# A running log-sum-exp over 4096 rows: Exp taken three chunks ahead of Ln, the last totals and the last store moved, small DMAs issued by GpSimd

## The chip, the core and the metric

The kernel runs on one core of one Trainium2 chip. The metric is device time in microseconds (us), the median of several runs. TensorE is called PE, VectorE DVE, ScalarE ACT, GpSimd POOL and SyncE SP, as in the profile.

## What is computed

The input x is 4 batches of 4096 rows of 4128 numbers (float32). Row t of the output is the log-sum-exp of rows 0 to t of the same batch, element by element:

```python
out[:, 0, :] = x[:, 0, :]
for t in range(1, S):
    mx = np.maximum(out[:, t - 1, :], x[:, t, :])
    out[:, t, :] = mx + np.log(np.exp(out[:, t - 1, :] - mx) + np.exp(x[:, t, :] - mx))
```

The kernel computes it as Ln of the running sum of Exp(x). That is good only as long as the sums stay in range, so it also works out a flag from the totals of all columns; only if the flag is 0 is everything done again by a slow general path. With these inputs the general path is not run.

## The kernel before

**Steps.** A batch's 4096 rows are cut into steps of 384 rows (3 rows for each of 128 partitions) and one of 256 rows (2 for each partition): ten of the one and one of the other, the short one first in batch 0 and last in the others. There are 44 steps, 0 to 43; the last one is short. A step is loaded into a buffer `xt` of 128 x 3 x 4128 by one DMA, worked on in place, and stored by one DMA. There are four buffers (`BUFS`). All loads (L87) and stores (L90) are issued by SyncE, in this order: loads 0 to 3, store 0, store 1, load 4, store 2, load 5 and so on, and at the end stores 41, 42 and 43. A load waits until the store of the step that had its buffer has landed.

**Chunks.** The columns of a step are worked on in four chunks, three of 1024 and one of 1056. The 176 chunks are numbered through. Each passes these operations:

- `exp` (L108, ACT): Exp of all its rows, in place.
- `sums` (L112, DVE): adds each partition's first row to its second and the second to the third.
- `head` (L119, PE): a matrix product with a triangle of ones (`excl`) gives each partition the sum of the partitions before it, added in PSUM (`base`) to what earlier steps left there. For the fourth chunk `head_rest` (L127, L129) does so in three pieces, with the earlier steps' sum from `carry`.
- `add` (L143) or `add_rest` (L136), DVE: adds that base to all rows.
- `pass_on` (L152, PE): puts the last partition's last row, the running total, into `base` for the next step; for the fourth chunk `keep` (L148, DVE) copies it to `carry`.
- `ln` (L164, ACT): Ln in place. It has to wait for `pass_on` or `keep`, which still read the sums.
- `total` (L159, DVE): after the last step of a batch, a chunk's totals are summed into a column of `part`.

**Order.** The order on every engine is written out by hand (`manual_schedule`), in one loop over the chunks. Round g does `sums` and `head` of chunk g + 1, `add` and `pass_on` of chunk g, `exp` of chunk g + 2, and `ln` of chunk g; behind the fourth chunk of a step stand its store and a later load. The rounds after the last step of a batch also hold the totals of the chunk before. So ScalarE alternates Exp of a chunk with Ln of the second chunk before it, and every engine takes its instructions strictly in order.

**The small loads.** Four DMAs, issued by ScalarE (L183), bring row 0 of each batch into a tile `first`, 32 partitions for each batch; at half of the loop its Exp(-x) is summed into the last column of `part` (L217).

**The end.** `part` is summed (L226), the partitions by a matrix product (L228), and compared with a limit (L229). All engines read the flag (L284) and branch (L285). The general path (L250 to L268) has its loads and stores on SyncE.

Of the kernel before, what the change touches and what calls it, by code (L numbers as in the profile page):

```python
# [7 lines left out]
FP32 = mybir.dt.float32  # L8
INT32 = mybir.dt.int32
ACT = mybir.ActivationFunctionType  # L10
AX = mybir.AxisListType
ALU = mybir.AluOpType
P = 128
R = 3
CH = 1024
MM = 512
BUFS = 4
HI = 96
LIMIT = float(2 ** 40)
STEPS = 15  # L20


def _constants(nc, pool):

    def triangle(base, name):
        t = pool.tile([P, P], FP32, name=name)
        nc.gpsimd.memset(t, 1.0)
        nc.gpsimd.affine_select(
            out=t, in_=t, pattern=[[1, P]], compare_op=ALU.is_ge,
            fill=0.0, base=base, channel_multiplier=-1,  # L30
        )
        return t

    excl = triangle(-1, "excl")
    pick = pool.tile([P, P], FP32, name="pick")
    nc.gpsimd.memset(pick, 0.0)
    nc.gpsimd.affine_select(  # L37
        out=pick, in_=pick, pattern=[[0, P]], compare_op=ALU.not_equal,
        fill=1.0, base=-(P - 1), channel_multiplier=1,
    )  # L40
    ones = pool.tile([P, 1], FP32, name="ones")
    nc.gpsimd.memset(ones, 1.0)
    return excl, pick, ones


def _fast(ctx, tc, x, out, flag):


    nc = tc.nc
    B, S, D = x.shape  # L50
# [6 lines left out]
    excl, pick, ones = _constants(nc, consts)  # L57
    xpool = ctx.enter_context(tc.tile_pool(name="xpool", bufs=BUFS))
    cpool = ctx.enter_context(tc.tile_pool(name="cpool", bufs=1))
# [1 line left out]
    prest = ctx.enter_context(tc.tile_pool(name="prest", bufs=2, space=bass.MemoryType.PSUM))  # L61

    carry = cpool.tile([P, rest], FP32, name="carry")
    q = P // B
    first = cpool.tile([P, D // q], FP32, name="first")
    part = cpool.tile([P, 4 * B + 1], FP32, name="part")
    every = cpool.tile([P, 1], FP32, name="every")
    nc.vector.memset(carry, 0.0)  # L68
# [5 lines left out]
    class Step:  # L74
        def __init__(self, b, row, r):
            self.b, self.row, self.r = b, row, r
            self.first = row == 0
            self.last = row + P * r == S
# [7 lines left out]
            self.xt = full[:, :self.r, :]  # L86
            nc.sync.dma_start(out=self.xt, in_=self.dram(x))  # L87

        def store(self):
            nc.sync.dma_start(out=self.dram(out), in_=self.xt)  # L90

    class Chunk:
        def __init__(self, step, c):
            self.t, self.c = step, c
            self.a = c * CH
            self.w = CH if c < 3 else rest
            self.end = c == 3
            self.q = {}

        def rows(self, lo, hi):  # L100
            return self.t.xt[:, lo:hi, self.a:self.a + self.w]
# [2 lines left out]
            return self.t.xt[:, j, self.a:self.a + self.w]  # L104

        def exp(self):
            rows = self.rows(0, self.t.r)
            nc.scalar.activation(rows, rows, ACT.Exp)  # L108

# [37 lines left out]
        def keep(self):  # L147
            nc.vector.tensor_copy(carry[HI:P, :], self.row(self.t.r - 1)[HI:P])  # L148

# [6 lines left out]
        def total(self):  # L156
            own = carry if self.end else base[self.c]
            i = 4 * self.t.b + self.c
            nc.vector.tensor_reduce(  # L159
                out=part[HI:P, i:i + 1], in_=own[HI:P, :self.w], axis=AX.X, op=ALU.add)  # L160

# [5 lines left out]
    for b in range(B):  # L167
        n = S // P
# [9 lines left out]
    chunks = [Chunk(s, c) for s in steps for c in range(4)]  # L178
    n = len(chunks)
    for s in steps[:BUFS]:  # L180
        s.load()
    for b in range(B):
        nc.scalar.dma_start(  # L183
            out=first[b * q:(b + 1) * q, :], in_=x[b, 0, :].rearrange("(q f) -> q f", q=q))
    stored = 0
    chunks[0].exp()
    chunks[1].exp()
    chunks[0].sums()
    chunks[0].head()
    for g, k in enumerate(chunks):  # L190
        after = chunks[g + 1] if g + 1 < n else None
        if k.end:
            k.add_rest(0)
            for i in range(2, len(subs)):
                k.head_rest(i)
            for i in range(1, len(subs)):
                k.add_rest(i)
            k.keep()
            if after:
                after.sums()  # L200
                after.head()
        else:
            after.sums()
            if after.end:
                after.head_rest(0)
                after.head_rest(1)
            else:
                after.head()
            k.add()
            k.pass_on()  # L210
        if g + 2 < n:
            chunks[g + 2].exp()
        k.ln()
        if g and chunks[g - 1].t.last:
            chunks[g - 1].total()
        if g == n // 2:
            nc.scalar.activation(  # L217
                first, first, ACT.Exp, scale=-1.0, accum_out=part[:, 4 * B:4 * B + 1])
        if k.end:
            k.t.store()  # L220
            if BUFS <= stored + BUFS - 1 < len(steps):
                steps[stored + BUFS - 1].load()
            stored += 1

    chunks[-1].total()
    nc.vector.tensor_reduce(out=every, in_=part, axis=AX.X, op=ALU.add)  # L226
    q = prest.tile([P, MM], FP32, name="q")
    nc.tensor.matmul(q[:1, :1], lhsT=every, rhs=ones, start=True, stop=True)  # L228
# [3 lines left out]
def _general(ctx, tc, x, out):  # L232

    nc = tc.nc
    B, S, D = x.shape
    q = P // B
    f = D // q
    assert P == B * q and D == q * f and (S - 1) % STEPS == 0
    one = ctx.enter_context(tc.tile_pool(name="one", bufs=1))
    state = one.tile([P, f], FP32, name="state")  # L240
    xs = one.tile([P, STEPS, f], FP32, name="xs")
    os = one.tile([P, STEPS, f], FP32, name="os")
    mx = one.tile([P, f], FP32, name="mx")
    two = one.tile([P, 2, f], FP32, name="two")

    def flat(t, b, first, n):
        return t[b, bass.ds(first, n), :].rearrange("t (q f) -> q t f", q=q)

    for b in range(B):
        nc.sync.dma_start(out=state[b * q:(b + 1) * q, :].unsqueeze(1), in_=flat(x, b, 0, 1))  # L250
    for b in range(B):
        nc.sync.dma_start(out=flat(out, b, 0, 1), in_=state[b * q:(b + 1) * q, :].unsqueeze(1))
    with tc.For_i(1, S, STEPS) as i:
        for b in range(B):
            nc.sync.dma_start(out=xs[b * q:(b + 1) * q], in_=flat(x, b, i, STEPS))
        for j in range(STEPS):
            own = state if j == 0 else os[:, j - 1, :]
            nc.vector.tensor_tensor(out=mx, in0=own, in1=xs[:, j, :], op=ALU.max)
            nc.vector.tensor_tensor(out=two[:, 0, :], in0=own, in1=mx, op=ALU.subtract)
            nc.vector.tensor_tensor(out=two[:, 1, :], in0=xs[:, j, :], in1=mx, op=ALU.subtract)  # L260
            nc.scalar.activation(two, two, ACT.Exp)
            nc.vector.tensor_tensor(
                out=two[:, 0, :], in0=two[:, 0, :], in1=two[:, 1, :], op=ALU.add)
            nc.scalar.activation(two[:, 0, :], two[:, 0, :], ACT.Ln)
            nc.vector.tensor_tensor(out=os[:, j, :], in0=mx, in1=two[:, 0, :], op=ALU.add)
        nc.vector.tensor_copy(state, os[:, STEPS - 1, :])
        for b in range(B):
            nc.sync.dma_start(out=flat(out, b, i, STEPS), in_=os[b * q:(b + 1) * q])  # L268


@with_exitstack
def kernel(
    ctx: ExitStack,
    tc: tile.TileContext,
    x: bass.AP,
    out: bass.AP,
):
    nc = tc.nc
    nc.scalar.preload_act_table_set("natural_log_exp_and_others")  # L279
    flags = ctx.enter_context(tc.tile_pool(name="flags", bufs=1))  # L280
    flag = flags.tile([1, 1], INT32, name="flag")
    with ExitStack() as inner:
        _fast(inner, tc, x, out, flag)
    good = nc.values_load(flag, min_val=0, max_val=1, skip_runtime_bounds_check_because="a comparison gives 0 or 1")  # L284
    with tc.If(good == 0, preferred_fallthrough_block=False):  # L285
        with ExitStack() as inner:
            _general(inner, tc, x, out)
# [30 lines left out]
```

## Time and profile before

| | us |
|---|---|
| median of 3 runs | 1272.1 (1271.65 to 1272.37) |
| profiled execution, device time | 1271.84 |
| its span, first to last instruction | 1270.1 |
| busy: DVE, ACT, PE | 1033.2, 929.3, 799.2 |
| load or store of a 3-row step | 6192 KB |
| load or store of a 2-row step | 4128 KB |

| work of a 3-row step | row | instructions x mean us |
|---|---|---|
| Exp | L108 | 3 x 2.75 and 1 x 2.83 |
| Ln | L164 | 3 x 2.76 and 1 x 2.83 |
| sums | L112 | 6 x 1.22 and 2 x 1.26 |
| add | L143 | 3 x 3.35 |
| add_rest | L136 | 2 x 1.75 and 1 x 0.25 |
| carry copy | L148 | 1 x 0.71 |

How to read the views: busy time is what an engine spent in instructions; the share of an engine says nothing of what sets the end. The DMA share is that of the 16 DMA engines together. In the rows of a timeline the bracket is the idle time of the engine before the instruction and what ended it. A row with x2 merges neighbours; its time runs from the start of the first to the end of the last. DMA issues (SPq) are instructions of the queue: they take 0.3 to 0.4 us, and the transfer lands later. PEclk is the share of TensorE's clock that was granted, 0.872 over the span.

### The profile page before, as it was taken

Reading aid. Unit: us, or ns where it says so; the run is one execution under the profiler, and the core shown is the slowest. Engines: PE = TensorE matmul, PEld = TensorE weight load, DVE = VectorE, ACT = ScalarE, POOL = GpSimd, SP = SyncE. Lnnn points to the kernel's source line nnn. Section 1 sums busy time; section 2 is a strip of 40 time slices with the busy share of each in tenths; the row PEclk is TensorE's granted clock in tenths of the full one; section 3 lists DMA queues with packets and bytes.
Section 4 is the critical chain, followed back from the end, with each engine's and each line's share of the span. In section 5 each row is a group of like instructions: output and inputs, shape, how many; then the busy total and the mean of one; then the engine's idle time right before and its main releaser. Section 6 shows DMA issues by size and latency. Waiting matters only on the chain.

```text
span 1270.1 us, 4844 instructions
## 1 busy us (share of the span) xinstructions
PE 799.2 (63%) x1562; PEld 304.9 (24%) x1562; DVE 1033.2 (81%) x664; ACT 929.3 (73%) x355; POOL 1.1 (0%) x9
## 2 busy tenths in 40 slices
PE   4566666656566766666656666666565766665574
PEld 1222222222122222222212222222221222222221
DVE  3888888888888887887788878788878888888775
ACT  4787787777777677767678777667866787677774
POOL 0000000000000000000000000000000000000000
PEclk9988888888888888887988998898978899798977
DMA  9999999999999999999999999999999999999987
GB/s 410 416 391 422 425 442 426 429 438 426 434 433 429 439 431 434 436 429 430 438 433 431 427 441 427 435 437 429 430 441 432 431 427 440 429 434 437 426 372 334
DMA packets 12890, 541.46 MB, mean 426 GB/s; under 512 B 1472, under 2 KB 1600, under 8 KB 1600
## 3 DMA queue, kind: packets, MB, share of 16 engines
q1 hardware_dynamic: 12672, 541.07, 98.9%
q8 instruction: 13, 0.21, 0.1%
q10 hardware_dynamic: 192, 0.07, 0.0%
q14 instruction: 13, 0.11, 0.0%
HBM read 270.60 MB, written 270.53 MB: 426 GB/s over the span
## 4 chain that ended last, share of the span: by engine, by line
DMA 42%; DVE 21%; ACT 20%; PE 10%; issue 6%; ACTq 0%; SPq 0%
DMA xt<-in_x_dram 24%; DMA out_dram<-xt 18%; ACT xt L164 10%; ACT xt L108 10%; DVE xt L143 9%; DVE xt L112 8%; PE base L152 5%; DVE xt L136 4%; PE base L119 3%; PE q L129 1%; DVE carry L148 1%; PE q L127 1%; DVE part L159 0%; ACTq L164 0%; ACT first L217 0%
## 5 line engine op out<-in xcount | busy, mean ns | idle before, releaser
L164 ACT ACTIVATE xt<-xt 128x3072 f32<-128x3072 f32 (+3 forms) x176 | 474.9, 2698 | 174.1 <-PE base L152 170.7
L108 ACT ACTIVATE xt<-xt 128x3072 f32<-128x3072 f32 (+3 forms) x176 | 473.6, 2692 | 152.3 <-DMA xt<-in_x_dram 152.2
L112 DVE TENSOR_TENSOR xt<-xt 128x1024 f32<-128x1024 f32 (+1 forms) x336 | 414.1, 1232 | 209.8 <-ACT xt L108 203.3
L119 PE MATMUL base<-xt,excl 128*128 128x512 f32 x528 | 356.4, 817 | 282.5 <-issue 146.9
L143 DVE TENSOR_TENSOR xt<-xt,base 128x3072 f32<-128x3072 f32 (+1 forms) x132 | 429.1, 3251 | 9.5 <-PE base L119 9.3
L152 PE MATMUL base<-xt,pick 128*128 128x512 f32 x528 | 263.7, 622 | 92.7 <-DVE xt L143 92.7
L119 PEld LDWEIGHTS base<-xt,excl 128*128 128x128 f32 x528 | 120.5, 250 | 476.0 <-issue 454.0
L129 PE MATMUL q<-xt,excl 128*128 128x512 f32 (+1 forms) x264 | 117.2, 530 | 77.9 <-DVE xt L112 54.1
L152 PEld LDWEIGHTS base<-xt,pick 128*128 128x128 f32 x528 | 95.2, 196 | 268.0 <-DVE xt L143 196.1
L136 DVE TENSOR_TENSOR xt<-xt,q 128x1536 f32<-128x1536 f32 (+1 forms) x132 | 153.7, 1214 | 1.6 <-PE q L129 1.4
L127 PE MATMUL q<-carry,pick 128*128 128x512 f32 (+1 forms) x240 | 101.5, 506 | 0.9 <-DVE xt L136 0.8
L129 PEld LDWEIGHTS q<-xt,excl 128*128 128x128 f32 x264 | 46.0, 200 | 140.2 <-issue 101.5
L127 PEld LDWEIGHTS q<-carry,pick 128*128 128x128 f32 x240 | 46.3, 197 | 63.9 <-issue 45.0
L148 DVE COPY carry<-xt 32x1056 f32<-32x1056 f32 x44 | 31.1, 706 | 1.5
L159 DVE TENSOR_REDUCE part<-base 32x1 f32<-32x1024 f32 x12 | 14.8, 1230 | 0.4
L159 DVE TENSOR_REDUCE part<-carry 32x1 f32<-32x1056 f32 x4 | 5.0, 1246 | 0.1
L228 PE MATMUL q<-ones,every 128*1 128x1 f32 x2 | 0.2, 164 | 4.1 <-DVE every L226 4.1
L279 ACT ACT_TABLE_LOAD x1 | 1.3, 1283 | 0.8 <-PEq L302 0.8
L68 DVE MEMSET carry<- 128x1056 f32 x1 | 0.9, 938 | 1.1 <-PEq L302 1.1
L228 PEld LDWEIGHTS q<-ones,every 128*1 128x1 f32 x2 | 0.1, 80 | 4.2 <-issue 4.2
L229 DVE TENSOR_SCALAR flag<-q 1x1 int32<-1x1 f32 x1 | 0.1, 147 | 0.4 <-PE q L228 0.4
L37 POOL TENSOR_SCALAR_AFFINE_SELECT pick<-pick 128x128 f32<-128x128 f32 x1 | 0.3, 297 | 0.0
(12 smaller groups left out, 1.9 us busy)
## 6 DMA issues: line engine op xcount, KB each, us to landing
xt<-in_x_dram SPq DMA_DIRECT2D x40, 6192.0 KB, 43.8
out_dram<-xt SPq DMA_DIRECT2D x40, 6192.0 KB, 33.0
xt<-in_x_dram SPq DMA_DIRECT2D x4, 4128.0 KB, 38.9
out_dram<-xt SPq DMA_DIRECT2D x4, 4128.0 KB, 28.4
first<-in_x_dram ACTq DMA_DIRECT2D x4, 16.1 KB, 10.7
```

What stands on the lines that cost most here:

```text
L108: nc.scalar.activation(rows, rows, ACT.Exp)
L112: nc.vector.tensor_tensor(out=self.row(j), in0=self.row(j - 1), in1=self.row(j), op=ALU.add)
L119: nc.tensor.matmul(base[self.c][:, s:s + MM], lhsT=excl, rhs=own[:, s:s + MM], start=t.first, stop=True, skip_group_check=True)
L127: nc.tensor.matmul(q[:, :w], lhsT=pick, rhs=carry[:, s:s + w], start=True, stop=False, skip_group_check=True)
L129: nc.tensor.matmul(q[:, :w], lhsT=excl, rhs=self.row(t.r - 1)[:, s:s + w], start=t.first, stop=True, skip_group_check=True)
L136: nc.vector.tensor_tensor(out=rows, in0=rows, in1=self.q[i][:, :w].unsqueeze(1).to_broadcast([P, t.r, w]), op=ALU.add)
L143: nc.vector.tensor_tensor(out=rows, in0=rows, in1=base[self.c].unsqueeze(1).to_broadcast([P, t.r, CH]), op=ALU.add)
L148: nc.vector.tensor_copy(carry[HI:P, :], self.row(self.t.r - 1)[HI:P])
L152: nc.tensor.matmul(base[self.c][:, s:s + MM], lhsT=pick, rhs=self.row(self.t.r - 1)[:, s:s + MM], start=True, stop=False, skip_group_check ...
L159: nc.vector.tensor_reduce(out=part[HI:P, i:i + 1], in_=own[HI:P, :self.w], axis=AX.X, op=ALU.add)
L164: nc.scalar.activation(rows, rows, ACT.Ln)
L279: nc.scalar.preload_act_table_set("natural_log_exp_and_others")
```

## The change

1. Exp runs three chunks ahead of Ln instead of two (`LAG`): round g issues the Exps up to chunk g + 3 that have not been issued. In the round of the last chunk of step 42 (g = n - 5) it goes only to g + 2, so that no Exp stands between there.
2. The totals of the last step's chunks are summed behind everything else on VectorE, not between the adds.
3. The last store is two DMAs: columns 0 to 2047 after Ln of the second chunk, columns 2048 to 4127 after Ln of the fourth.
4. The four small loads are issued by GpSimd; their tile has 8 partitions a batch (8 x 516) instead of 32 (32 x 129).
5. The DMAs of the general path are issued by GpSimd instead of SyncE.

The lines of the changed kernel are a few further on (L111 for L108, L167 for L164, L88 and L91 for L87 and L90).

```diff
+LAG = 3
...
-    q = P // B
-    first = cpool.tile([P, D // q], FP32, name="first")
+    q = 8
+    first = cpool.tile([B * q, D // q], FP32, name="first")
...
-        def store(self):
-            nc.sync.dma_start(out=self.dram(out), in_=self.xt)
+        def store(self, lo=0, hi=D):
+            nc.sync.dma_start(out=self.dram(out)[:, :, lo:hi], in_=self.xt[:, :, lo:hi])
...
     for b in range(B):
-        nc.scalar.dma_start(
+        nc.gpsimd.dma_start(
             out=first[b * q:(b + 1) * q, :], in_=x[b, 0, :].rearrange("(q f) -> q f", q=q))
...
-    chunks[0].exp()
-    chunks[1].exp()
+    for c in chunks[:LAG]:
+        c.exp()
...
-        if g + 2 < n:
-            chunks[g + 2].exp()
+        for c in chunks[g + 1:g + (LAG if g == n - 5 else LAG + 1)]:
+            if not c.done:
+                c.exp()
         k.ln()
-        if g and chunks[g - 1].t.last:
+        if g and chunks[g - 1].t.last and g < n - 4:
             chunks[g - 1].total()
...
-        if k.end:
+        if g == n - 3:
+            k.t.store(0, 2 * CH)
+        elif k.end and g == n - 1:
+            k.t.store(2 * CH)
+        elif k.end:
             k.t.store()
...
-    chunks[-1].total()
+    for c in chunks[-4:]:
+        c.total()
...
-        nc.sync.dma_start(out=state[b * q:(b + 1) * q, :].unsqueeze(1), in_=flat(x, b, 0, 1))
+        nc.gpsimd.dma_start(out=state[b * q:(b + 1) * q, :].unsqueeze(1), in_=flat(x, b, 0, 1))
```

The other DMAs of the general path change in the same way.

More of the change, by code (lines that the diff above doesn't have):

```diff
@@ L98, in __init__ @@
             self.q = {}
+            self.done = False
         def rows(self, lo, hi):
@@ L106, in exp @@
         def exp(self):
+            self.done = True
             rows = self.rows(0, self.t.r)
@@ L217, in _fast @@
             nc.scalar.activation(
-                first, first, ACT.Exp, scale=-1.0, accum_out=part[:, 4 * B:4 * B + 1])
-        if k.end:
+                first, first, ACT.Exp, scale=-1.0, accum_out=part[:first.shape[0], 4 * B:4 * B + 1])
+        if g == n - 3:
[3 more added lines that the diff above has]
+        elif k.end:
             k.t.store()
@@ L249, in _general @@
     for b in range(B):
-        nc.sync.dma_start(out=state[b * q:(b + 1) * q, :].unsqueeze(1), in_=flat(x, b, 0, 1))
+        nc.gpsimd.dma_start(out=state[b * q:(b + 1) * q, :].unsqueeze(1), in_=flat(x, b, 0, 1))
     for b in range(B):
-        nc.sync.dma_start(out=flat(out, b, 0, 1), in_=state[b * q:(b + 1) * q, :].unsqueeze(1))
+        nc.gpsimd.dma_start(out=flat(out, b, 0, 1), in_=state[b * q:(b + 1) * q, :].unsqueeze(1))
     with tc.For_i(1, S, STEPS) as i:
         for b in range(B):
-            nc.sync.dma_start(out=xs[b * q:(b + 1) * q], in_=flat(x, b, i, STEPS))
+            nc.gpsimd.dma_start(out=xs[b * q:(b + 1) * q], in_=flat(x, b, i, STEPS))
         for j in range(STEPS):
@@ L267, in _general @@
         for b in range(B):
-            nc.sync.dma_start(out=flat(out, b, i, STEPS), in_=os[b * q:(b + 1) * q])
+            nc.gpsimd.dma_start(out=flat(out, b, i, STEPS), in_=os[b * q:(b + 1) * q])
 @with_exitstack
```

## The prediction

> **What bounds the kernel now.** I read the page first, then SyncE's queue in order of time, then short windows at both ends, then ScalarE's and VectorE's rows there. Steps are numbered 0 to 43, chunks 0 to 175 (chunk = 4 x step + column chunk).
>
> The page: span, DMA tenths, and the queue that carries the loads and stores.
>
> ```profile
> span 1270.1 us, 4844 instructions
> ...
> DMA  9999999999999999999999999999999999999987
> ...
> q1 hardware_dynamic: 12672, 541.07, 98.9%
> ```
>
> One queue is busy for 98.9% of the span. VectorE (81%) and ScalarE (73%) are not the bound: the chain names them only because they wait beside a full queue. What a faster order of Exp and Ln can win is thus the time in which that queue is empty. The windows of 1 us (last two columns: DMA share, GB/s) show where:
>
> ```profile
> 67.00:68.00 1.00, 1.00 (x3) 0.21 (x1) 1.00 (x1) 1.00 (x1) 0.00 (x0) 0.50 0.01 0
> 68.00:69.00 1.00, 1.00 (x2) 0.61 (x2) 0.37 (x2) 1.00 (x2) 0.00 (x0) 0.50 0.00 0
> ...
> 1238.00:1239.00 1.00, 0.69 (x2) 0.45 (x3) 1.00 (x2) 1.00 (x1) 0.00 (x0) 1.00 0.00 0
> 1239.00:1240.00 1.00, 1.00 (x4) 0.23 (x2) 1.00 (x1) 1.00 (x2) 0.00 (x0) 1.00 0.00 0
> ...
> 1256.00:1257.00 1.00, 0.00 (x0) 0.00 (x0) 0.97 (x2) 0.50 (x1) 0.00 (x0) 0.50 0.00 0
> ```
>
> A packet counts where it starts, so a zero says that none was begun. Three holes: near 68, near 1239, near 1256. SyncE's rows say what ends each, a store that could not be issued sooner:
>
> ```profile
> 40.86 27.92 SPq L90 DMA_DIRECT2D out_dram<-xt  x2
> 68.89 0.37 SPq L87 DMA_DIRECT2D xt<-in_x_dram  x1
> ...
> 1239.77 17.09 SPq L90 DMA_DIRECT2D out_dram<-xt  x2
> ```
>
> The second store of the first row is step 1's, at 68.44; the last row holds step 42's at 1239.77 and step 43's at 1256.53. In between the queue is never empty: the rows of the loads and stores issued at 1156.6, 1182.0 and 1185.9 land 43.8, 33.0 and 38.9 us later, that is at 1200.4, 1215.0 and 1224.8: 14.6 and 9.8 us apart, for 6192 and 4128 KB. These spacings are the price of a queued transfer.
>
> **Exp three chunks ahead: the hole near 68.** By the spacings step 1's store would land 14.6 us after step 0's (40.86 + 27.0 = 67.9), at 82.5. It lands at 68.44 + 17.0 = 85.4, 2.9 late. The hole itself is some 2.0 us (no start between 67 and 69). I take 2.3.
> Does the change close it? VectorE waits for Exp on the way:
>
> ```profile
> 28.89 1.26 DVE L112 TENSOR_TENSOR xt<-xt 128x1056 f32<-128x1056 f32 x1 [2.77 <-ACT xt L108]
> ...
> 39.02 2.49 DVE L112 TENSOR_TENSOR xt<-xt 128x1024 f32<-128x1024 f32 x2 [0.98 <-ACT xt L108]
> ...
> 52.37 2.55 DVE L112 TENSOR_TENSOR xt<-xt 128x1056 f32<-128x1056 f32 x2 [1.94 <-ACT xt L108]
> ```
>
> With Exp a chunk earlier these 5.7 us go; step 1's store moves from 68.44 to 62.7, or to 65.5 if only the last two waits go. It has to be issued by about 66.1: no packet starts after 66.4, the last ones take 1.2 us and end at 67 or so, and the store of 1239.77 has its first packets 0.8 us after the issue (windows of 0.1 us). So both ends close the hole. Gain 2.0 to 2.9, value 2.3; 0 if the store stays behind 68. What is late next is the queue itself: step 2's store (95.85) is already issued before load 4 is through.
>
> **The same change in the middle.** It adds a wait. Exp of the next step's first chunk now stands before Ln of this step's second chunk, not third. It waits for a load, and behind it in ScalarE stand three Ln and the step's store. Before, the store went 10.9 us after the landing (1200.4 to 1211.3); two more instructions (an Exp and a Ln, 2.75 + 2.76) make it 16.4. Its data could not start sooner than 1224.8 (29.2 after landing in a full step), so at least 8 us of cover are left and the cost is 0. SyncE's next load stands behind that store and is issued some 2 us later, with a whole load still queued before it: 0. VectorE and ScalarE lose no work and gain none. The period stays 29.3 us a step, which is the DMA's.
>
> **The hole near 1239.** Load 43 lands at 1224.8, with the first gain at 1222.5. The built order of ScalarE after it is Exp 172, Ln 169, Exp 173, Ln 170, Ln 171, then step 42's store. By the means of these forms, 1.90 + 2.76 + 1.90 + 2.76 + 2.83 = 12.2: the store goes at 1234.7. Ln 171 needs VectorE's carry copy, at 1233.09 before; the wait of 3.51 us for Exp 171 at 1223.48 goes, since Exp 171 now stands ahead of Ln 168, so 1229.6. Before, two Ln waited 4.03 and 4.54 us for PE here, and an Exp of step 43 stood ahead of Ln 171. The slowest ring ends step 41's store by its landing, 1211.3 + 28.9 = 1240.2, less 2.3: 1237.9. So the store is in the queue 3 us early.
>
> **The hole near 1256.** After step 42's store: Exp 174, Exp 175, Ln 172, Ln 173, then the first part. Before, from the carry copy at 1233.09 to the end of Ln 173 it was 1249.0 - 1233.1 = 15.9 us; from 1229.6 that gives 1245.5. The second part follows the last Ln, before at 1256.5, 23.4 after the carry copy, now less the totals of two chunks that stood between adds (2 x 1.23): 1229.6 + 21 = 1250.6. Step 42's store is through at 1237.9 + 14.6 = 1252.5 and the first part at 1257.4. Both parts are queued 7 us ahead. Worth: step 42's store landed at 1239.8 + 18.0 = 1257.8, 17.6 after step 41's where the spacing is 14.6, and step 43's at 1256.5 + 11.2 = 1267.7, 9.9 after that. Together 3.1 over the spacings; the windows show 0.8 of hole for the slowest ring and 1.8 to 2 for all. I take 3.0.
>
> **The totals.** Four of 1.23 us now stand behind the last carry copy instead of between. That delays the flag (1257.6) by 2.5 us, while the carry copy comes some 6 us sooner by the shift worked out above: about 1254, 8 us ahead of the last landing: 0.
>
> **Two column parts.** The rows that move shrink from 33 KB (two whole rows of a partition) to 8 KB, 32 packets a ring for 8. Nothing here shows 8 KB rows of a store. The nearest rows are the page's small queues: q8 with 13 packets of 16 KB, whose 0.1% of 16 engines (0.05 to 0.15) is 0.8 to 2.3 us each, in rings that share with a busy queue. At that rate 264 KB a ring would take 13 to 38 us for 9.8. At the other end, nothing: 8 KB is the sixth part of rows that run at full rate, and the transfer is the same. I take +0.2, as q8's packets had to share and these do not. Below nothing is excluded, as no byte goes.
> The trace shows no fixed price for a queued DMA: the landings above are as far apart as their bytes. The Trainium skill, "DMA: Bandwidth & Descriptors", section "Anatomy of one DMA — SWDGE (gpsimd) path", speaks against it with about 2.0 us fixed for each DMA; by that the forecast would be 2 us higher, 1268.3.
>
> **DMAs by GpSimd.** The four small loads leave ScalarE's queue before 3.1 us, where it waits for load 0 until 13.45 anyway, and are read at mid-span: 0. The general path is not run, but its DMAs decide where SyncE waits for all stores. Now it does so inside the If (8.8 us, below), and branches on to the end block only then:
>
> ```profile
> SPq L285 <- SPq L285: 8.8, 1, 8.8
> ...
> L285 SPq EVENT_SEMAPHORE  x8: 17/17/17, 1258.8 to 1268.0; - x8
> ...
> L313 SPq EVENT_SEMAPHORE  x10: 17/28/28, 1268.6 to 1270.0; - x10
> ```
>
> In the changed program SyncE's empty arm has no such waits; they are in the end block, which it reaches early. From the landing at 1267.7 to the first wait of the end block at 1268.6 is 0.9; I take 0.8 of it as gone (0 to 0.9). On the other side four register moves go from SyncE to GpSimd, ahead of the barrier at the start; SyncE's take 0.03 us each, 0.07 apart: +0.2 (0 to 0.3). GpSimd's own waits at the end are for loads long landed.
>
> **Sum.** -2.3 - 3.0 - 0.8 + 0.2 + 0.2 = -5.7 on the profiled execution's 1271.84 (span 1270.1 and 1.7 around it): 1266.1. That execution lies 0.26 under the median of the runs, 1272.1, so I forecast 1266.3.
>
> **Rivals.**
> *One hole stays.* The clock of PE was 0.5 from 64 to 70 and in 1228 to 1230; where it falls elsewhere, a pass of 2.0 us becomes 3.5 or so. For: the hole near 68 closes by as little as 0.5 us. Against: the other two have 3 and 7. Price: 2.3 back, 1268.6.
> *The slowest ring takes it.* The end is that of the slowest of 16 rings, and they drift: step 41's store landed at 1240.2, yet at 1236 to 1238 the share was about 0.2, so most rings had ended 4 us before. Instruction loads (q8, q14) share the rings; one of 16 KB on the slowest costs up to 2 us, and a kinder spread gives as much. 1268.2, or 1264.3.
> *The change doesn't do what it says in time*: stores are hidden anyway, or another transfer is late, and the end stays within 2.5 us: 1270.5. For: 98.9% leaves 14 us at most to win in all, and I claim over a third of it.
> *Slower.* The parts of the last store run at the small packets' price. Place: the last 9.8 us, with nothing beside them. From 9.8 to 18.2 us the gain of 5.9 and the bound of 2.5 are eaten; that is 14.5 KB a microsecond and ring against 26.9. At q8's middle, 1.5 us for 16 KB, they take 24 us: 1280. Against: q8 shared its rings.
>
> **Chances.** Forecast (1265 to 1267.6) 0.50; one hole stays 0.12; slowest ring unkind 0.12, kind 0.11; no gain 0.11; slower 0.04. A measurement of this kernel tells about 0.2% from no change, 2.5 us, so faster means under 1269.6: 0.85; same 0.11; slower 0.04. For the range I leave out the slower case, most of the no-gain case and the far end of the kind one: 1263.5 to 1270.0.
>
> **What would show it.** Right: step 1's store issued before 66 and no empty window near 68; step 42's before 1236; both parts before 1251; no zero windows until the last bytes; SyncE's waits for the stores in the end block, and the end some 1.5 us after the last landing instead of 2.35. Wrong: a store still late at 68; landings of the two parts more than 5.2 us apart; a slowest ring further behind the fastest than now.

## The result, and the profile after

| | before | after |
|---|---|---|
| median of 6 runs each, us | 1271.88 (1269.66 to 1272.37) | 1264.32 (1264.18 to 1264.69) |
| profiled execution, us | 1271.84 | 1264.18 |
| its span, us | 1270.1 | 1262.7 |

The ratio is 0.9944 (95% interval 0.9932 to 0.9957): faster by 0.6%. The forecast was 1266.3, with a range of 1263.5 to 1270.0. The direction and the places of the gain were right; the sum was 2.0 us short, and one of its terms was mis-sized by nearly half. So the measured time lies in the range, but below the 1265 to 1267.6 that the prediction gave the forecast itself.

The page of the changed kernel, the lines that answer to those of before: span, the DMA tenths, the queue of loads and stores, and the groups of Exp (L111) and Ln (L167; L108 and L164 before), whose last column is the idle time ahead of them and what ended most of it.

```profile
span 1262.7 us, 4848 instructions
...
DMA  9999999999999999999999999999999999999998
...
q1 hardware_dynamic: 13072, 541.07, 99.4%
...
L111 ACT ACTIVATE xt<-xt 128x3072 f32<-128x3072 f32 (+3 forms) x176 | 473.6, 2693 | 306.2 <-DMA xt<-in_x_dram 306.2
...
L167 ACT ACTIVATE xt<-xt 128x3072 f32<-128x3072 f32 (+3 forms) x176 | 473.3, 2690 | 19.9 <-PE base L155 19.9
```

The queue's share went from 98.9% to 99.4% with the same bytes. Ln's waits for PE fell to 19.9 us from 170.7, Exp's waits for loads rose to 306.2 from 152.2: nearly all of it was exchanged, as neither engine is the bound.

SyncE's issues near the first hole, and the DMA windows of 1 us there and at the places of the two later holes (last two columns: DMA share, GB/s):

```profile
64.51 0.34 SPq L91 DMA_DIRECT2D out_dram<-xt  x1
67.99 0.34 SPq L88 DMA_DIRECT2D xt<-in_x_dram  x1
```

```profile
67.00:68.00 1.00, 0.77 (x2) 0.00 (x0) 1.00 (x1) 0.22 (x1) 0.00 (x0) 0.93 1.61 694
68.00:69.00 1.00, 0.69 (x2) 0.45 (x3) 1.00 (x2) 0.00 (x0) 0.00 (x0) 1.00 1.03 446
...
1230.00:1231.00 1.00, 1.00 (x3) 0.48 (x2) 0.95 (x1) 1.00 (x1) 0.00 (x0) 0.50 0.46 198
1231.00:1232.00 1.00, 1.00 (x3) 0.19 (x1) 1.00 (x1) 1.00 (x1) 0.00 (x0) 0.96 0.12 50
...
1238.00:1239.00 1.00, 1.00 (x3) 0.38 (x2) 1.00 (x2) 0.00 (x0) 0.00 (x0) 1.00 1.61 694
...
1256.00:1257.00 1.00, 0.00 (x0) 0.00 (x0) 0.00 (x0) 0.00 (x0) 0.00 (x0) 0.50 0.96 399
1259.00:1260.00 1.00, 0.00 (x0) 0.00 (x0) 0.00 (x0) 0.00 (x0) 0.00 (x0) 0.50 0.14 58
1260.00:1261.00 1.00, 0.00 (x0) 0.00 (x0) 0.00 (x0) 0.00 (x0) 0.00 (x0) 0.50 0.04 17
```

Step 1's store goes at 64.51, not 68.44, and the windows at 68, 1238 and 1256 are full. (A ring is the part of the queue on one of the 16 DMA engines; in the trace every load and store has 16 landings, one for each ring.) What is left: at 1230 to 1232 the fast rings have nothing to do (the slowest does), and in the last two microseconds only a few rings still work, at the end a single one.

VectorE's rows that waited for Exp before (2.77, 0.98 and 1.94 us) have no bracket now; a wait of 1.16 us for PE, between them, is new:

```profile
26.59 1.25 DVE L115 TENSOR_TENSOR xt<-xt 128x1056 f32<-128x1056 f32 x1
...
33.48 4.88 DVE L115 TENSOR_TENSOR xt<-xt 128x1024 f32<-128x1024 f32 x4
39.52 3.35 DVE L146 TENSOR_TENSOR xt<-xt,base 128x3072 f32<-128x3072 f32 x1 [1.16 <-PE base L122]
...
48.45 2.54 DVE L115 TENSOR_TENSOR xt<-xt 128x1056 f32<-128x1056 f32 x2
```

At the end, SyncE's issues of step 42's store and the two parts (1232.39, 1241.63 and 1248.63, merged in one row), and the waits for the stores, now in the end block (L322), with first and last start:

```profile
1232.39 16.77 SPq L91 DMA_DIRECT2D out_dram<-xt  x3
```

```profile
L322 SPq EVENT_SEMAPHORE  x14: 17/28/28, 1253.5 to 1262.6; - x14
```

**Where the time went.** By the landings (always of the last ring) in the two traces:

| place | forecast | measured |
|---|---|---|
| up to load 43 and step 41's store | -2.3 (hole near 68) + 0.2 (start) | -4.3 (1224.80 to 1220.53; 1240.23 to 1235.97) |
| from there to the last landing | -3.0 + 0.2 (8 KB rows) | -2.15: step 42's store 14.65 after step 41's instead of 17.54 (-2.89), the last bytes 10.69 after that instead of 9.95 (+0.74) |
| from the last landing to SyncE's last instruction | -0.8 | -1.0 (1.34 instead of 2.35) |
| sum | -5.7 | -7.4 |

The time outside the span, 1.7 us before and 1.5 after, adds another 0.25.

So the question for the experiments: why was the hole near 68, some 2 us long, worth 4.3?

**A second view of the hole.** The trace also holds every packet of the queue. It does not name the packet's ring; where single rings are spoken of, they were followed by packets that start where another ended. A packet of 49.5 KB (the three rows of one partition) nearly always takes 1.83 us. In the trace of before, two groups of 16 packets stand out: around the landings of step 1's store and of load 4, where the rings go from storing to loading and back, they take 2.53 and 2.86 us in the mean. Below, *excess* is the time of packets over the usual time of their size, summed over a stretch and divided by the 16 rings. From 75 to 105 us it is 2.04 us a ring before and 0.49 after. Averaged over some 22 us around the two changes of direction it shows in the windows as a rate, with the DMA share at 1, so not as idle time. Before:

```profile
80.00:102.00 22.00, 14.19 (x28) 5.33 (x26) 20.39 (x15) 16.47 (x7) 0.00 (x0) 0.84 1.01 395
```

After:

```profile
78.00:100.00 22.00, 14.24 (x30) 5.64 (x29) 20.34 (x14) 18.42 (x8) 0.00 (x0) 0.84 1.01 429
```

395 GB/s against 429 over 22 us is 1.7 us. A zero in the DMA share finds the hole; this part of its price it does not show. In before, the 16 rings begin step 1's store within 0.15 us (69.29 to 69.43), since all waited for it; after, they come from step 0's store one by one, over 0.73 us.

### The profile page after: what moved, and what is told of

Same layout as the page of the kernel before. It is cut to its first block, busy times and chain, and to the rows that moved or that the text cites. A ratio compares the mean times of both kernels' runs of the same rounds, so it can differ in the third digit from the quotient of the medians.

```text
span 1262.7 us, 4848 instructions
## 1 busy us (share of the span) xinstructions
PE 785.6 (62%) x1562; PEld 305.1 (24%) x1562; DVE 1028.2 (81%) x664; ACT 921.5 (73%) x355; POOL 3.3 (0%) x13
## 3 DMA queue, kind: packets, MB, share of 16 engines
q1 hardware_dynamic: 13072, 541.07, 99.4%
## 4 chain that ended last, share of the span: by engine, by line
DMA 37%; DVE 33%; ACT 19%; issue 7%; PE 3%; SPq 0%; ACTq 0%
DMA xt<-in_x_dram 37%; DVE xt L146 16%; DVE xt L115 11%; ACT xt L167 11%; ACT xt L111 8%; DVE xt L139 4%; PE base L122 2%; PE base L155 1%; DVE carry L151 1%; DVE part L162 1%; SPq L91 0%; PE q L132 0%; PE q L130 0%; ACTq L167 0%; PE q L237 0%
## 5 line engine op out<-in xcount | busy, mean ns | idle before, releaser
L111 ACT ACTIVATE xt<-xt 128x3072 f32<-128x3072 f32 (+3 forms) x176 | 473.6, 2693 | 306.2 <-DMA xt<-in_x_dram 306.2
L122 PE MATMUL base<-xt,excl 128*128 128x512 f32 x528 | 363.9, 831 | 365.5 <-DVE xt L115 330.5
L115 DVE TENSOR_TENSOR xt<-xt 128x1024 f32<-128x1024 f32 (+1 forms) x336 | 413.4, 1232 | 202.9 <-ACT xt L111 196.6
L167 ACT ACTIVATE xt<-xt 128x3072 f32<-128x3072 f32 (+3 forms) x176 | 473.3, 2690 | 19.9 <-PE base L155 19.9
L155 PE MATMUL base<-xt,pick 128*128 128x512 f32 x528 | 266.4, 628 | 89.9 <-DVE xt L146 89.9
L132 PE MATMUL q<-xt,excl 128*128 128x512 f32 (+1 forms) x264 | 106.2, 487 | 2.8 <-DVE xt L115 2.8
L130 PE MATMUL q<-carry,pick 128*128 128x512 f32 (+1 forms) x240 | 94.2, 474 | 1.5 <-DVE xt L139 1.3
L162 DVE TENSOR_REDUCE part<-base 32x1 f32<-32x1024 f32 x12 | 14.6, 1228 | 0.3
```

Of the source, the lines that this page charges most:

```text
L115: nc.vector.tensor_tensor(out=self.row(j), in0=self.row(j - 1), in1=self.row(j), op=ALU.add)
L122: nc.tensor.matmul(base[self.c][:, s:s + MM], lhsT=excl, rhs=own[:, s:s + MM], start=t.first, stop=True, skip_group_check=True)
L130: nc.tensor.matmul(q[:, :w], lhsT=pick, rhs=carry[:, s:s + w], start=True, stop=False, skip_group_check=True)
L132: nc.tensor.matmul(q[:, :w], lhsT=excl, rhs=self.row(t.r - 1)[:, s:s + w], start=t.first, stop=True, skip_group_check=True)
L155: nc.tensor.matmul(base[self.c][:, s:s + MM], lhsT=pick, rhs=self.row(self.t.r - 1)[:, s:s + MM], start=True, stop=False, skip_group_check ...
L162: nc.vector.tensor_reduce(out=part[HI:P, i:i + 1], in_=own[HI:P, :self.w], axis=AX.X, op=ALU.add)
```

## Experiments

All are the changed kernel with one thing altered, unless said otherwise. Ratios are to the kernel before, timed beside them.

### Is the hole's price more than its length?

Theory A: its length, 2.0, and slow packets at the next changes of direction, because the rings start again in step. Theory B: its length alone, the rest is from other edits.

**early_two**: the lead is three chunks, but two in the first eight rounds.

```diff
-    for c in chunks[:LAG]:
+    for c in chunks[:2]:
...
-        for c in chunks[g + 1:g + (LAG if g == n - 5 else LAG + 1)]:
+        for c in chunks[g + 1:g + (LAG if g == n - 5 or g < 8 else LAG + 1)]:
```

> The changed kernel, but Exp runs only two chunks ahead in the first eight rounds (steps 0 and 1), as before; everything later is unchanged. So step 1's store should go at about 68.5 again and the empty stretch of 2.0 us near 68 be back, with nothing else touched. In the two traces the landings of the slowest ring differ by 2.6 us at step 1's store but by 3.8 to 4.3 us from load 4 on. Theory A: the other 1.7 us belong to the hole too, because the 16 rings start again in step and then all change from stores to loads and back at the same time (in the trace of before, the packets at these two changes near 83 and 98 take 2.5 and 2.9 us in the mean instead of 1.83; in the changed kernel 1.87 and 2.1). It expects +3.8 to +4.3 us on the changed kernel's 1264.3, that is 1268.1 to 1268.6, and load 4 landing at about 102. Theory B: the hole costs only its length, and the rest came from the other edits (small loads through GpSimd, another place of the instruction loads). It expects +2.0 to +2.6, 1266.3 to 1266.9, and load 4 landing at about 100.8.

1269.50 (1268.72 to 1274.86, 10 runs), 0.9984 [0.9974, 0.9993]: 5.2 above the change, beyond both theories. But the hole came out longer than the one it was to bring back: in its trace the store goes at 70.72, the rings stand still for 4.0 to 4.7 us instead of 1.8 to 2.5, and load 4 lands at 105.87, 7.3 later than in the change. That execution is the slowest of the ten (1274.86), and how long the hole was in the other nine is not known, so this run's time does not tell A from B. The packets do: the excess from 75 to 105 is 2.18 a ring.

```profile
41.37 29.70 SPq L91 DMA_DIRECT2D out_dram<-xt  x2
71.16 0.38 SPq L88 DMA_DIRECT2D xt<-in_x_dram  x1
```

```profile
69.00:70.00 1.00, 0.77 (x1) 0.00 (x0) 0.97 (x2) 1.00 (x1) 0.00 (x0) 0.50 0.00 0
```

**lag_only**: the kernel before, with the lead of three and nothing else.

```diff
-    chunks[0].exp()
-    chunks[1].exp()
+    for c in chunks[:LAG]:
+        c.exp()
...
-        if g + 2 < n:
-            chunks[g + 2].exp()
+        if g + LAG < n:
+            chunks[g + LAG].exp()
```

> The kernel before with one part of the change alone: Exp three chunks ahead, everywhere; one store at the end, totals between the adds, small loads and general path as before. By the terms: the hole near 68 closed (-4.2 by theory A, -2.5 by theory B) and the hole near 1239 closed (-0.8), while the hole near 1256 stays in part, since the last Ln comes some 2.5 us later than in the changed kernel (store at about 1251, step 42's store through at 1250), worth 1 to 2 us; the waits for the stores stay inside the If (0.8). Sum from 1271.9: theory A 1266 to 1267, theory B 1268 to 1269. A rival that gives the gain to the other parts of the change (stores, totals, GpSimd) expects 1270 or more.

1265.44 (1264.83 to 1266.13, 4 runs), 0.9956 [0.9939, 0.9972]. The lead alone brings 5.9 of the 7.6 us, a little more than A said (the kernel before took 1271.35 beside it, 0.5 less than beside the change). With none of the other edits in it, B's "the rest is from other edits" falls. Store 1 goes at 64.21, the last two stores at 1233.02 and 1246.52: the one before the last ring is through with step 41's store (1234.6), the other before any is through with step 42's (1248.9):

```profile
1233.02 13.83 SPq L91 DMA_DIRECT2D out_dram<-xt  x2
```

**no_lag**: all of the change but the lead, which is two again.

```diff
-LAG = 3
+LAG = 2
```

> The changed kernel with Exp two chunks ahead throughout; totals behind all adds, the store in two parts and the DMAs by GpSimd as changed. Both early and late holes that the lead closes should be back: near 68 (theory A 4.2, theory B 2.5) and near 1239 (0.8 for the slowest ring). What stays gained: the hole near 1256 (about 2) and the end block (0.8), less 0.2 at the start and 0.3 for the rows of 8 KB. Sum from 1271.9: 1269.5. If this and the run of the lead alone add up to the whole (7.6 us below 1271.9), the parts do not depend on each other; if their gains sum to more, they close the same hole.

1269.38 (1268.73 to 1271.95, 10 runs), 0.9990 [0.9980, 0.9999]: as expected. Its gain of 2.0 and the lead's 5.9 add up to 7.9, near the whole. The hole near 68 is back: the rings stand still for 2.2 to 2.9 us, the excess from 75 to 105 is 2.07, and load 43 lands at 1225.47, even later than before and 4.9 later than in the change:

```profile
67.00:68.00 1.00, 1.00 (x2) 0.34 (x1) 0.97 (x2) 1.00 (x1) 0.00 (x0) 0.50 0.01 0
68.00:69.00 1.00, 1.00 (x3) 0.28 (x2) 0.60 (x1) 1.00 (x2) 0.00 (x0) 0.50 0.00 0
```

**hole_mid**: a hole made by hand where there is none. 17 Exps of an idle tile (1.06 us each) stand ahead of the last Ln of step 20, so that its store goes 19 us later.

```diff
+        if g == 4 * 20 + 3:
+            for _ in range(17):
+                nc.scalar.activation(idle, idle, ACT.Exp, scale=0.0)
         k.ln()
```

> The changed kernel with 17 idle Exp instructions of 128 x 1024 on a zeroed tile ahead of the last Ln of step 20 (some 0.93 us each, 15.8 in all); they compute nothing that is used. Step 20's store goes 15.8 us later, that is some 32 us after load 21's landing, where its data could have begun 29.2 after it: a hole of about 3.8 us for the slowest ring (a us more or less, as ScalarE has some idle time), and more for the others, in the middle of a stream that is full otherwise. Theory A (rings that start in step pay at the next two changes of direction): the time rises by the hole and 1.5 to 2 us more, 1269.5 to 1270.3, and the packets at the next two changes take 2.5 us or more in the mean. Theory B (a hole costs its length): 1268.1, and those packets take 1.9 to 2.1 as elsewhere.

1272.51 (1271.57 to 1273.33, 10 runs), 1.0010 [1.0001, 1.0020]: 8.2 above the change, more than either theory. The store goes at 627.68; the slowest ring stands still for 3.95 us (624.55 to 628.50), as meant, the fastest for some 10, the 16 for 7.9 in the mean:

```profile
622.00:625.00 3.00, 0.00 (x0) 0.00 (x0) 0.00 (x0) 2.94 (x4) 0.00 (x0) 0.50 0.04 17
625.00:628.00 3.00, 0.00 (x0) 0.00 (x0) 0.00 (x0) 3.00 (x2) 0.00 (x0) 0.50 0.00 0
...
640.00:662.00 22.00, 14.73 (x25) 5.26 (x26) 21.71 (x14) 12.16 (x8) 0.00 (x0) 0.84 0.95 372
```

The changed kernel in the same window:

```profile
640.00:662.00 22.00, 11.19 (x22) 4.24 (x22) 17.12 (x12) 12.23 (x8) 0.00 (x0) 0.82 1.02 442
```

Behind the hole the rings begin within 0.16 us, and the groups of packets at the next two changes of direction (642 and 658) take 2.49 and 2.82 us in the mean. The excess from 600 to 900 is 3.8 a ring against 0.5. In this trace the two add up: 7.9 us of standing still and 3.3 of slow packets in the mean of the rings, and the mean landing of load 43 is 11.3 later, counted from load 22; the last ring, which stood still least, lands it 9.2 later. So the slow packets come with a hole anywhere, not only at the start. A holds in kind, but it expected 1.5 to 2 us of slow packets. B falls by the packets; by the time it falls only if the hole's length is the slowest ring's 3.95, as the mean pause of 7.9 alone would nearly give the 8.2. The next run decides that.

### Whose pause counts, and do the rings have to be in step?

**hole_short**: the same with 12 idle Exps, so that only the faster rings run dry.

> The change with 12 idle Exps ahead of the last Ln of step 20 instead of 17: step 20's store goes 5.4 us sooner than with 17, at about 622.3, its first packets at 623.1. The slowest ring is then still busy with load 23 (to 624 or so), the fastest has stood still since 618.6. Theory A1 (only the slowest ring's pause counts, and the rings that start together leave it alone): 1264.3 to 1264.8. Theory A2 (rings that start in step make slow packets for the slowest one too): 1265.3 to 1267. A theory by which the share of empty time counts, whichever ring has it (2.5 us in the mean of the rings): 1266.8.

1268.85 (1268.40 to 1272.33, 11 runs), 0.9979 [0.9970, 0.9988]: 4.5 above the change, more than all three.

```profile
618.00:623.00 5.00, 0.00 (x0) 0.00 (x0) 0.00 (x0) 4.97 (x4) 0.00 (x0) 0.53 0.39 168
```

The window ends where 14 of the rings start again within 0.15 us (623.06 to 623.21). The slowest ring went from load 23 to the store at 624.55 without a pause, and still its packets at the next two changes took 2.11 and up to 2.80 us instead of 1.83: the last ring lands the load behind that store 16.2 us after it, where the spacing is 14.6. The excess from 600 to 900 is 3.3 against 0.5. So A2 is right in kind: a pause of the fast rings costs the slowest ring too, through the packets that follow. The pause is 2.4 us in the mean of the rings, so that a hole does not just cost its mean length either (1266.8). In this trace load 43 lands 4.3 later than in the change's, of which 0.9 was there before the hole. Three rings did not pause and had slow packets all the same (0.6 to 2.3 us of excess at the two changes); that rules out a slowness that only a ring which has paused would have.

**stagger**: hole_mid, with a DMA of 8 rows ahead of the store, to start half of the rings later.

```diff
+            if g == 4 * 20 + 3:
+                nc.sync.dma_start(out=steps[24].dram(out)[:8, :2, :], in_=k.t.xt[:8, :2, :])
             k.t.store()
```

> The kernel with the hole in the middle (17 idle Exps ahead of the last Ln of step 20) and one more DMA on SyncE's queue just ahead of step 20's store: 8 rows of 33 KB, that is one packet of 1.22 us on 8 of the 16 rings, written to rows of step 24 that its own store writes again later. So after the same hole half of the rings begin step 20's store some 0.8 us behind the other half, instead of all 16 within 0.16 us. In the kernel with the hole the packets around the next three changes of direction (near 642, 658 and 683) took 2.49, 2.82 and 2.07 us in the mean for 1.83. Theory A (these packets are slow because the rings change direction at one time): they fall to 2.2 or less, and the time is 1272.5 + 1.2 (the packet) - 1 to 2: 1271.2 to 1272.7, no slower than without the added DMA. Rival (they are slow because the queue has stood still, or because it changes direction at all): the packets stay at 2.4 to 2.8, and the time is 1273.3 to 1273.8.

1276.95 (1275.63 to 1277.57, 5 runs), 1.0039 [1.0026, 1.0053]: a miss. The 8 packets, each from another partition of the first eight and alone on its ring, took 4.9 to 5.6 us instead of 1.22, so that half of the rings began 4.3 to 5.2 us late:

```profile
627.00:633.00 6.00, 3.31 (x4) 1.51 (x5) 4.56 (x3) 6.00 (x4) 0.00 (x0) 0.50 1.04 300
```

The first half began step 20's store within 0.1 us, the second within 0.9. The excess at the two changes was 0.65 and 0.97 a ring, against 0.88 and 1.16 in hole_mid. Two halves 4 us apart are a fifth less slow than 16 together. So "all 16 at one time" is not needed. At the first of the two changes the halves differ: the last packets of the store took 2.60 to 2.70 us in the half that was in step to 0.1 us, all eight of them, and 1.83 to 1.85 in the half that was up to 0.9 apart, though it had stood still too. That speaks for being in step as the cause, and against standing still, and so does the change itself: at 82 us, with its rings 0.73 us apart and no pause, it has an excess of 0.14 where before has 0.84. A hole after which all rings are spread was not tried, so the cause of the slow packets is argued, not shown.

### What do the other edits bring beside the lead?

Theory C: the lead alone fills the queue at the end. Theory D: the split and the moved totals are needed, as the prediction had it for the hole near 1256.

**old_tail**: one last store, totals between the adds, three chunks ahead in every round. **one_store**: only the split undone. **totals_between**: only the totals undone.

```diff
-        if g == n - 3:
-            k.t.store(0, 2 * CH)
-        elif k.end and g == n - 1:
-            k.t.store(2 * CH)
-        elif k.end:
+        if k.end:
```

```diff
-        if g and chunks[g - 1].t.last and g < n - 4:
+        if g and chunks[g - 1].t.last:
...
-    for c in chunks[-4:]:
-        c.total()
+    chunks[-1].total()
```

> The change with its end put back: one last store instead of two column parts, the totals of the last step between the adds again, and Exp three chunks ahead in every round, also that of step 42's last chunk. The lead and the DMAs by GpSimd stay. Theory C (the lead alone fills the queue at the end; the other edits there only cost): the last store goes at about 1246.5, as in the kernel with the lead alone, before step 42's store is through (1248.9 to 1250.6), so nothing is lost, and its 33 KB rows save 0.3: 1264.0; worked out from the kernel with the lead alone instead, 1265.44 - 1.0 (end) + 0.23 (start) = 1264.7. Theory D (the split and the moved totals are needed, as the prediction's step for the hole near 1256 has it): 1265.8 or more.

> The change with one last store instead of two parts, all else kept. Theory C: the single store goes where the second part went, at 1248.6, with its first packets at 1249.4. Most rings have then been through with step 42's store for about half a microsecond (1248.9), the slowest not (1250.6): 1264.0 to 1264.3. Theory D: the rings stand still until the last Ln, and all 16 start again in step: 1265.5 or more.

> The change with the totals of the last step's chunks between the adds again. Three of 1.23 us then stand ahead of the last add: the last Ln and the second part's issue go back by at most 3.7 us, from 1248.6 to 1252.3, still ahead of the first part's landing (1253.4 in the median, 1255.5 in the last ring): 1264.3, no change. If the place of the totals matters, as the change assumes: 1265.5 to 1268.

| | us (5 runs each) | ratio |
|---|---|---|
| old_tail | 1264.63 (1263.52 to 1264.88) | 0.9944 [0.9930, 0.9957] |
| one_store | 1264.29 (1263.76 to 1264.88) | 0.9942 [0.9929, 0.9956] |
| totals_between | 1264.41 (1263.74 to 1264.97) | 0.9942 [0.9928, 0.9955] |
| the change | 1264.32 (1264.18 to 1264.69) | 0.9944 [0.9932, 0.9957] |

C, in all three. In old_tail the last two stores go at 1234.54 and 1247.72; step 42's store is through at 1250.5 (most rings) to 1252.5.

```profile
1234.54 13.51 SPq L91 DMA_DIRECT2D out_dram<-xt  x2
```

In one_store the last store goes at 1250.08, and most rings, done at 1248.6, do stand still for some 2 us; no change of direction follows, and it lands at 1262.43 against 1261.31. In the profiled execution that is 1.1 us, 0.4 of it given back as its end is 0.92 behind the landing; the medians show none of it.

**old_issuers**: the small loads by ScalarE and the general path's DMAs by SyncE, as before. **first_act**: only the small loads by ScalarE. **lead_and_general**: old_tail with the small loads by ScalarE, so that of the change only the lead and the general path's DMAs by GpSimd are left.

```diff
-        nc.gpsimd.dma_start(
+        nc.scalar.dma_start(
             out=first[b * q:(b + 1) * q, :], in_=x[b, 0, :].rearrange("(q f) -> q f", q=q))
```

> The change with the four small loads on ScalarE's queue and the general path's DMAs on SyncE's, as before. By the prediction's steps the waits for the stores go back into the If arm, and the end comes 1.0 us later behind the last landing (2.35 for 1.35), the start 0.23 sooner: 1265.1. Rival: where SyncE waits costs nothing in itself, as the end block's work follows the last landing either way: 1264.1, with the last landing 0.2 sooner.

> The change with the four small loads on ScalarE's queue again; the general path's DMAs stay with GpSimd. If the register moves ahead of the start barrier belong to the general path's DMAs, the first load still goes at 1.04, and the time is 1264.3 as with the whole change; if they belong to the small loads, 0.81 and 1264.1. In both cases the end stays 1.35 us behind the last landing.

> Of the whole change only the lead (in every round) and the general path's DMAs on GpSimd: one last store, totals between the adds, small loads by ScalarE. If the other edits bring nothing beside the lead, as the runs so far say (1264.29 to 1264.63 with any of them undone), this gives 1264.3, between 1263.9 (33 KB rows at the end, no wait for the small loads) and 1264.7. If one of them covers for another, so that two have to go before it shows: 1265.5 or more.

old_issuers: 1264.75 (1264.28 to 1265.60, 5 runs), 0.9948 [0.9934, 0.9962]. In its trace the end is 2.04 behind the last landing (1.34 in the change), and the waits for the stores are back in the If arm (L294), with the end block's behind them; the first load goes at 0.81. The 0.4 in the medians is no more than their spread, so that part is shown by the trace alone:

```profile
L294 SPq EVENT_SEMAPHORE  x8: 17/17/17, 1252.4 to 1261.0; - x8
```

```profile
L322 SPq EVENT_SEMAPHORE  x10: 17/28/28, 1261.6 to 1262.8; - x10
```

first_act: 1264.07 (1263.76 to 1265.90, 5 runs), 0.9943 [0.9930, 0.9957]; the first load still goes at 1.04, so the register moves ahead of the barrier belong to the general path's DMAs. lead_and_general: 1264.60 (1264.21 to 1265.64, 5 runs), 0.9944 [0.9930, 0.9957]: nothing was hidden under anything else. None of these versions beats the change by more than the spread; the simplest of them is as fast.

## Why the prediction was right, and where it was not

- **The hole near 68** (-2.3): right in mechanism, mis-sized. Step 1's store went at 64.51, inside the 62.7 to 65.5 worked out. The step took a hole to cost its length, or the lateness of the next landing (2.0 to 2.9). It measured 4.3 at load 43. The length is 1.8 to 2.5 us by ring (to 69.3 or 69.4 from 66.9 to 67.5); the rest is in the packets at the two changes of direction behind it, 2.04 us a ring before and 0.49 after. In the mean of the rings that is 2.2 and 1.55, together the 3.7 by which the mean landing of load 43 moved; the last ring moved by 4.3. The other kernels with a hole there have 2.07 and 2.18, the seven others with the lead from the start and no hole made by hand 0.2 to 0.8. The trace of before had those packets, and the landing of load 4 at 102.33, 16.9 after step 1's store where the spacing is 14.6; the prediction looked no further than the store.
- **The same change in the middle** (0): right. From load 6 to load 43 the gain stays between 4.2 and 4.3.
- **The holes near 1239 and 1256** (-3.0): both went. Step 42's store follows step 41's by 14.65, the spacing. But the step gave the gain to the issue orders of the end, and the lead alone has it: any of those edits can be undone for nothing. They do have an effect where the lead is missing: no_lag is 2.0 faster than before, of which 1.0 is the end block. In the sum this stretch, with the 8 KB rows, came to -2.15 instead of -2.8.
- **Totals** (0): right; the flag is at 1251.5, 10 us ahead of the last landing.
- **Two column parts** (+0.2): the 8 KB packets take 0.319 us, the 33 KB ones 1.240 for four times the bytes: 0.009 x 32 packets a ring, 0.3. The Trainium skill's fixed 2.0 us for each DMA ("DMA: Bandwidth & Descriptors", "Anatomy of one DMA — SWDGE (gpsimd) path") did not show: the change and one_store are 0.03 us apart. That section's figure is a fit for DMAs that GpSimd issues; these stores are SyncE's. The rest of the +0.74 at the end is in the last ring: an 8 KB instruction load at 1256.9 (0.33 us) and the packet behind it, 0.79 for 0.32. That ring ends 2.8 us behind most of the others, but 2.2 of this it brought along (step 42's store landed in it at 1250.62, in most at 1248.4): it was still busy with step 41's store while the others waited. Such 8 KB loads now fall into the last store (1256.9, 1257.5 and 1258.4), where before two came at 1269.1 and 1270.4, behind the branch; that they hold the end block's code is likely by their times, not shown.
- **End** (-0.8): -1.0 in the trace. **Start** (+0.2): +0.23 at the first issue, gone by the landing of step 0's store (67.92 for 67.88); first_act shows that it comes with the general path's DMAs, not with the small loads.
- **Rivals**: none took place. The chance for "slowest ring kind", 1264.3, has the right number by another cause, so that it fits by luck. Small packets at q8's price did not come: the parts' last bytes were 10.69 us behind step 42's, not 18.
- **Signs**: all of those named for being right came true. Of those for error, the parts landed 5.77 us apart in the last ring, over the 5.2 named; in the median ring 5.14. It was the instruction load and the packet behind it, not the packets' size. The other, a slowest ring further behind the fastest than now, came true at the very end (2.8 us for 0.2 in the last store), but not at step 41's store (7.0 for 8.4).

What stays open: how far apart rings have to be to pass a change of direction freely; why the second change behind a hole is slow too, when the rings are no longer so close (they land at 659.97 to 660.60 in hole_mid); and why the profiled execution of early_two (1274.86, its highest) and stagger's have 2.1 to 2.2 us a ring of slow packets between 900 and 1100, where no pause precedes them and the other twelve have 0.4 to 0.8.

## What to carry to other kernels

When one DMA queue is the bound, a hole in it can cost more than its length, wherever it lies: here holes of 2.2 and 2.4 us in the mean of the rings cost 4.3 and 4.5, and one of 4.0 in the slowest ring, 7.9 in the mean, cost 8.2. The queue that starts again makes slow packets at its next changes between loading and storing. So read the rate behind a hole as well as the hole, by landings against the usual spacing over the next two or three transfers. And before shaving the end, look whether one lead in the order of work already keeps the queue fed there: of five edits, one carried 5.9 of 7.6 us, and moving the waits out of the branch about one more, by the traces.

## What the runs showed of the hardware that was not expected

- At the first two changes between stores and loads after the rings have started in step (0.15 us), packets take up to 3.6 us for 1.83. Where the rings are 5.5 us apart, they take nearly the usual time: in the changed kernel the excess from 600 to 900 us is 0.54 a ring, over some 20 changes. At 82 us the eleven kernels with the lead from the start have their rings 0.45 to 0.75 us apart, and an excess of 0.05 to 0.17.
- The rings start in step and drift apart as the run goes on: at 620 us the last ring of the changed kernel is 5.5 us behind the first, at 1230 us 7.0. A hole brings them together again.
- Eight packets of 33 KB from eight neighbouring partitions, one to a ring, took 4.9 to 5.6 us each; in stores that use all 128 partitions the same size takes 1.22.
- SyncE's waits at the end take some 0.06 us each, in a fixed order. Where the last store's wait stands last in it (old_tail), the end comes 0.91 us after the landing; where eight stand behind or with it (the change), 1.34.
- A kernel with such a hole varied more: before took 1268.8 to 1274.7 in 55 runs, the eight kernels without one 1263.5 to 1266.1 in 40. One run of the former says little.
